# Eight blocks of a matrix-vector product move from TensorE to GpSimd, and three small tiles grow to 64 bytes

## The chip, the cores and the metric

One core of a Trainium2 chip runs the whole program. The metric is the device time of one execution in microseconds, the median of several runs. A profiled execution gives the trace, from which every row below is read.

## The reference

Two transformer blocks run one after the other on 512 tokens of width 1024; the first also carries 256 context tokens. What matters here is the first block's start:

```python
mod_lat = jnp.split((jax.nn.silu(c) @ w_mod[l] + b_mod[l])[:, None, :], N_MOD, axis=-1)   # w_mod: 1024 x 9216
mod_ctx = jnp.split(jax.nn.silu(c_ctx) @ w_mod[l] + b_mod[l], N_MOD, axis=-1)
x = ffn_sub(x, mod_lat[0:3], ...); s_ctx = ffn_sub(s_ctx, mod_ctx[0:3], ...)        # first feed-forward
h_lat = modulate(rmsnorm(x, norm2_w[l]), mod_lat[3], mod_lat[4])                    # and the same for the context
x = x + mod_lat[5] * lat_mix                                                       # after the mixer
x = ffn_sub(x, mod_lat[6:9], ...)                                                  # second feed-forward
```

So 9 vectors of 1024 numbers come from two matrix-vector products with one 37.7 MB matrix; vectors 0 to 2 are wanted by the first feed-forward, 3 and 4 just behind it, 5 after the mixer, 6 to 8 by the second feed-forward. The mixer holds an mLSTM scan and an HGRN2 scan. The second block holds a state-space mixer, sparse attention and a mixture of 32 experts.

## The kernel before

Everything is fp32. A large product is done as three fp32r matmuls (`mm3`, L210 to L212): the weights are split into a rounded part `whi` and a rest `wlo` (`wsplit`, L191 and L192), the activations into `lath`/`latl`, `ctxh`/`ctxl` and `hh`/`hl`. A feed-forward (`ffn`) takes the hidden width of 2816 in 22 slices of 128, in eight groups of 2, 2, 3, 3, 3, 3, 3, 3. A slice has two weight loads for its first product (outputs `pppa`, 512 columns for the latents, 256 for the context) and one for its second (outputs `pppb`). After each group one function of the list `fill` is called.

A block of the matrix-vector product (`matvec`, four columns of 128 outputs) loads 2 MB of weights in four DMAs on SP's queue, runs 8 fp32 matmuls with 32 columns of weights (L265; the trace has two records for each), copies the result out and turns and sums it with 4 matmuls (L275, eight records). `mod` has 18 such blocks, named here by their first column: 0 to 12 before the first feed-forward, 16 and 20 in `begin`, 24 to 36 after groups 0 to 3 of it, and 40 to 68 in the list `self.fill`, which also has four blocks of `w_ada_2`. From that list two are taken behind the feed-forward (`FT`, L2458), one ahead of each of the four heads of the mLSTM scan (`FB[0]`, L807), one in each of the four HGRN2 fronts (`FB[1]`, L940) and two at the end of these (`FB[2]`, L528). These come through the ordinary weight buffers `wraw`; the ones in the feed-forward through `mraw` (`MR` = 6 buffers).

Instructions are written in program order and a planner orders each engine's queue from that order and from modelled times; on the chip each queue then runs strictly in order. A DMA on SP's queue that waits for a buffer holds every DMA behind it.

Tiles are stacked: a pool takes addresses (bytes within a partition) upward from the pool below it, each tile rounded up to 32 bytes, and the pools `wp` (`wraw`, `whi`, `wlo`) and `tp` come down from the other end. In this program `whi` and `wlo` lie at 186336, 190432, ... and 198624, ..., all 32 above a multiple of 64. The constants begin at 16512, `eps` (4 bytes, takes 32) lies at 17760, and everything opened later lies on top: `lath` at 21504, `latl` at 37888, `ctxh` at 54272, all multiples of 64. `hh` and `hl` lie at multiples of 64 in the first feed-forward (125120, 128192, ...), and at 32 above one in the second (123104, 126176, ...), because there they sit on another stack, with `inv` (4 bytes, takes 32) under them. The last tile under the expert weights `ew` (123904, a multiple of 64) is `frs` (16 bytes, takes 32).

GpSimd has the lower halves of some normalised blocks (`norm_block`, L355 and L356, for k in 0, 3, 6) and work of the scans.

Of the kernel before, what the change touches and what calls it, by code (L numbers as in the profile page):

```python
# [10 lines left out]
F32 = mybir.dt.float32  # L11
# [5 lines left out]
OP = mybir.AluOpType  # L17
# [23 lines left out]
class Kern:  # L41
# [60 lines left out]
    def setup(self):  # L102
        nc, cst = self.nc, self.cst
        self.ident = cst.tile([128, 128], F32, name="ident")
        nc.sync.dma_start(self.ident, self.i["k_ident"])
        self.ones = cst.tile([128, 128], F32, name="ones")
        nc.vector.memset(self.ones, 1.0)
        self.sel4 = cst.tile([128, 32], F32, name="sel4")
        nc.sync.dma_start(self.sel4, self.i["k_sel4"])
        self.eps = cst.tile([128, 1], F32, name="eps")  # L110
        nc.vector.memset(self.eps, 1e-6)
        self.tiny = cst.tile([128, 1], F32, name="tiny")
        nc.vector.memset(self.tiny, 7.8e-20)

# [101 lines left out]
    mva = False  # L216
# [25 lines left out]
    def mvrows(self, p):  # L242
        if self.mvp is None:
            rows = self.tp.tile([128, 512], F32, name="mvr", tag="mvr", bufs=1)
            self.nc.scalar.copy(rows, p)
        else:
            rows = self.mvp.tile([128, 512], F32, name="mvs", bufs=2)
            (self.nc.scalar.copy if self.mva else self.nc.vector.tensor_copy)(rows, p)
        return rows

    def matvec(self, dst, w, sc, n, c0, nb, bias, tag=None):

# [225 lines left out]
HGL = 420  # L478
ZB = 6
EARLY = 200  # L480
FB = (1, 1, 2)
LV = [64, 32, 16, 8, 4, 2, 1]
QSC = 0.5 * 128 ** -0.5

# [641 lines left out]
class Mix2:  # L1126
# [3 lines left out]
    def rope_tables(self, i, pool, cosd, sind):  # L1130

        nc = self.nc
        inv = pool.tile([128, 1], F32, name="inv")
        nc.sync.dma_start(inv, i["k_invf"])
        pos = i["positions_2"][0]
        pf = self.tmp("posf")
        if pos.dtype == I32:
            raw = self.tmp("pos0").bitcast(I32)
            nc.sync.dma_start(raw[0:1, :], pos[None, :])
            nc.vector.tensor_copy(pf[0:1, :], raw[0:1, :])  # L1140
        else:
            p32 = pos.bitcast(I32)
            for r in range(2):
                raw = self.tmp("pos%d" % r).bitcast(I32)
                nc.sync.dma_start(raw[0:1, :], p32[r * 512:(r + 1) * 512][None, :])
                nc.vector.tensor_copy(pf[0:1, r * 256:(r + 1) * 256], raw[0:1, 0:512:2])
        p = self.pt("pb")
        nc.tensor.matmul(p, self.ones[0:1, :], pf[0:1, :], start=True, stop=True)
        ang = self.tmp("ang")
        nc.vector.tensor_scalar(ang, p, inv, None, op0=OP.mult)  # L1150
        MG = 12582912.0
        C1, C2, C3 = 6.28125, 1.9350051879882812e-03, 3.019916050561733e-07
        k = self.tmp("kk")
        nc.vector.tensor_scalar(k, ang, 1.0 / (2 * math.pi), MG, op0=OP.mult, op1=OP.add)
        nc.vector.tensor_scalar(k, k, MG, None, op0=OP.subtract)
        for c in (C1, C2, C3):
            nc.vector.scalar_tensor_tensor(ang, k, -c, ang, op0=OP.mult, op1=OP.add)

        ab = self.tmp("ab")
        nc.scalar.activation(ab, ang, AF.Abs)  # L1160
        s = self.tmp("sn")
        nc.vector.tensor_scalar(s, ab, -1.0, 3.14159274101257324, op0=OP.mult, op1=OP.add)
        nc.vector.scalar_tensor_tensor(s, s, -8.74227766e-08, ab, op0=OP.add, op1=OP.min)
        nc.scalar.activation(s, s, AF.Sin)
        sg = self.tmp("sg")
        nc.scalar.activation(sg, ang, AF.Sign)
        nc.vector.tensor_mul(s, s, sg)
        nc.sync.dma_start(sind, s)
        nc.vector.tensor_scalar(ab, ab, -1.0, math.pi / 2, op0=OP.mult, op1=OP.add)
        nc.scalar.activation(ab, ab, AF.Sin)  # L1170
        nc.sync.dma_start(cosd, ab)
# [786 lines left out]
class Moe:  # L1958
# [271 lines left out]
    def finish(self, mo, yac, yg, fg, out):  # L2230

        nc = self.nc
        ss = mo.tile([128, 4, 2], F32, name="fss")
        for c in range(4):
            for f in range(2):
                fs = slice(f * 512, f * 512 + 512)
                j = self.tmp("fj")
                nc.scalar.activation(j, yac[:, c, fs], AF.Square, accum_out=ss[:, c, f:f + 1])
                (nc.vector if f else nc.gpsimd).tensor_tensor(yg[:, c, fs], yac[:, c, fs], fg[:, fs], op=OP.mult)  # L2239
        r = mo.tile([128, 4], F32, name="frs")  # L2240
        nc.vector.tensor_add(r, ss[:, :, 0], ss[:, :, 1])
        nc.scalar.activation(r, r, AF.Ln, bias=self.eps, scale=1.0 / D)
        nc.scalar.activation(r, r, AF.Exp, scale=-0.5)
        for c in range(4):
            if c % 2:
                nc.scalar.activation(yg[:, c, :], yg[:, c, :], AF.Copy, scale=r[:, c:c + 1])
            else:
                nc.vector.tensor_scalar(yg[:, c, :], yg[:, c, :], r[:, c:c + 1], None, op0=OP.mult)
            nc.sync.dma_start(out[c * 128:(c + 1) * 128, :], yg[:, c, :])
# [73 lines left out]
LATE = 1500  # L2323
FT = (2,)
M0 = 16
MR = 6
FN = 6
FA = 2
MA = (0, 1)
# [22 lines left out]
class Top:  # L2352
# [41 lines left out]
    def first(self, i, b1, lat, mrg, xd, x1d, cosd, sind, row):  # L2394
        nc, tc, cst = self.nc, self.tc, self.cst
        wm = i["w_mod"][0]
# [22 lines left out]
        with tc.tile_pool(name="xp", bufs=1, reuse_waits="tile") as xp:  # L2419
# [5 lines left out]
            a, b = A("sA"), A("sB")  # L2425
# [8 lines left out]
            ada = b1.tile([128, 16, 1], F32, name="ada")  # L2434
            vec, g1 = {}, A("sG")

            def begin():
                mm(16)
                mm(20)
                gate(2, 0.5, 2, g1)  # L2440
                self.bada = self.columns("c", [("b", i["b_ada_2"][0], 48)])["b"]
                self.sc2 = self.silu_cols([i["c_2"]], "2")
                vec.update(self.columns("b", [("l0", i["hg_lb_logits"][0].rearrange("a b -> (a b)"), 8),
                                              ("l1", i["hg_lb_logits"][1].rearrange("a b -> (a b)"), 8),
                                              ("hgw", i["hg_norm_w"][0], 4), ("mlcw", i["ml_conv_w"][0], 36),
                                              ("mlcb", i["ml_conv_b"][0], 4)]))
                self.lower_bounds(vec["l0"], vec["l1"], vec)
                self.fill = [lambda b=b: mm(b) for b in range(40, 72, 4)]
                self.fill += [lambda b=b: self.matvec(ada[:, b:b + 4], i["w_ada_2"][0], self.sc2, 1, b * 128, 4,
                                                      self.bada[:, b:b + 4]) for b in range(0, 16, 4)]  # L2450
            g = g1
            with tc.tile_pool(name="mw", bufs=1, reuse_waits="tile") as self.mvp, \
                    tc.tile_pool(name="act", bufs=1, reuse_waits="tile") as self.act:
                self.ffn(i["ffn1_w1"][0], i["ffn1_w2"][0], hi, lo, [(0, L, xT, g[:, 0]), (L, C, xc, g[:, 1])],
                         self.ends(xT, g[:, 0]) + [(L, C, xc, g[:, 1])],
                         begin, [lambda b=b: mm(b) for b in range(24, 40, 4)])
            self.mvp = None
            self.fillers(FT[0])  # L2458
            a, b = scales(3, "n2")
# [116 lines left out]
```

## Time and profile before

| | us |
|---|---|
| median of 3 runs | 2839.8 (2837.2 to 2843.13) |
| profiled execution, its own time | 2847.28 |
| its span from first to last instruction | 2845.5 |
| TensorE (PE) busy | 2684.1 (94%) |
| VectorE (DVE) busy | 1553.9 (55%) |
| ScalarE (ACT) busy | 995.2 (35%) |
| GpSimd (POOL) busy | 280.4 (10%) |

Times of rows count from the start of the span. An engine's busy time is the union of its instructions; a matmul's end is modelled, so two matmuls in a row overlap in the list, and what one costs is the distance from its start to the next start. "L12" is line 12 of the kernel. In brackets behind a row of the order of time stands the idle time before the instruction, and what ended it.

### The profile page before, as it was taken

What the parts mean: (1) busy time and instruction counts of PE and PEld (TensorE: products, weight loads), DVE (VectorE), ACT (ScalarE), POOL (GpSimd) and SP (SyncE); (2) the same over time, 40 slices, a digit from 0 to 9 for tenths busy, and PEclk for the clock granted to TensorE, in tenths of its full rate; (3) what the DMA queues carried; (4) which work ended last, traced back from release to release, by engine and by line L of the source; (5) the groups of instructions that cost most, each with busy time, mean ns of one, the idle gap of its engine ahead of it and who ended that gap; (6) DMA issues with size and microseconds to landing.
All of it is one profiled execution on the core that took longest, in us unless ns stands there. A gap on an engine that the chain in (4) does not pass through costs nothing. (4 is left out here: it accounts for less than half of the span.)

```text
span 2845.5 us, 40809 instructions
## 1 busy us (share of the span) xinstructions
PE 2684.1 (94%) x16161; PEld 2052.9 (72%) x16162; DVE 1553.9 (55%) x3022; ACT 995.2 (35%) x1787; POOL 280.4 (10%) x319
## 2 busy tenths in 40 slices
PE   7999999999998887999999899999999989969997
PEld 5788888888887765678788678777777767854443
DVE  6333333338367895554435756676666664454444
ACT  5211112225235663422223424555444443231112
POOL 2000000003001220100000101121122220000000
PEclk8999999999999998999999999999999999979999
DMA  7422222134333228732333433201234367269995
GB/s 261 149 89 67 59 61 66 46 97 118 94 102 103 64 83 263 260 96 82 105 95 103 135 87 95 80 13 43 78 104 119 97 195 242 74 245 377 379 378 203
DMA packets 340996, 384.66 MB, mean 135 GB/s; under 512 B 20793, under 2 KB 251581, under 8 KB 340546
## 3 DMA queue, kind: packets, MB, share of 16 engines
q1 hardware_dynamic: 338498, 373.62, 40.7%
q0 software_dynamic: 2304, 8.39, 0.8%
q8 instruction: 129, 2.11, 0.3%
q14 instruction: 65, 0.53, 0.1%
HBM read 352.33 MB, written 29.63 MB: 134 GB/s over the span
## 5 line engine op out<-in xcount | busy, mean ns | idle before, releaser
L191 ACT CAST whi<-wraw 128x1024 fp32r<-128x1024 f32 x277 | 285.9, 1042 | 756.7 <-PE pppa L211 329.3
L210 PE MATMUL pppa<-lath,whi 128*128 128x512 f32 (+4 forms) x1344 | 523.1, 390 | 19.5 <-ACT lath L1833 5.4
L211 PE MATMUL pppa<-latl,whi 128*128 128x512 f32 (+3 forms) x1344 | 519.7, 387 | 5.1 <-DVE latl L358 3.0
L212 PE MATMUL pppa<-lath,wlo 128*128 128x512 f32 (+3 forms) x1344 | 513.2, 384 | 0.0
L192 DVE TENSOR_TENSOR wlo<-wraw,whi 128x1024 fp32r<-128x1024 f32 (+1 forms) x273 | 332.4, 1224 | 252.0 <-ACT whi L191 247.4
L210 PEld LDWEIGHTS pppa<-lath,whi 128*128 128x128 f32 (+3 forms) x1344 | 253.0, 188 | 87.4 <-ACT whi L191 11.9
L211 PEld LDWEIGHTS pppa<-latl,whi 128*128 128x128 f32 (+2 forms) x1344 | 252.6, 188 | 65.4 <-DVE latl L358 5.4
L212 PEld LDWEIGHTS pppa<-lath,wlo 128*128 128x128 f32 (+2 forms) x1344 | 252.1, 188 | 55.5 <-issue 2.5
L211 PE MATMUL pppb<-hl,whi 128*128 128x512 f32 (+1 forms) x576 | 195.3, 341 | 0.0
L210 PE MATMUL pppb<-hh,whi 128*128 128x512 f32 (+1 forms) x576 | 193.1, 344 | 0.0
L212 PE MATMUL pppb<-hh,wlo 128*128 128x512 f32 (+1 forms) x576 | 191.5, 341 | 0.0
L416 DVE SCALAR_TENSOR_TENSOR xT<-pppb,sG,xT 128x512 f32<-128x512 f32 (+1 forms) x144 | 96.7, 689 | 137.7 <-PE pppb L212 137.5
L396 DVE TENSOR_TENSOR hf<-sg,pppa 128x256 f32<-128x256 f32 (+1 forms) x68 | 39.7, 584 | 234.6 <-PE pppa L212 233.3
L210 PE MATMUL pppf<-lath,whi 128*128 128x512 f32 x320 | 128.9, 403 | 5.9 <-ACT lath L1833 2.2
L210 PE MATMUL pppa<-ctxh,whi 128*128 128x256 f32 (+1 forms) x440 | 125.1, 284 | 7.9 <-DVE W L919 7.9
L211 PE MATMUL pppf<-latl,whi 128*128 128x512 f32 x320 | 128.3, 401 | 0.8 <-DVE latl L1834 0.7
L2137 PE MATMUL pppa<-ew,xg 128*64 128x512 f32 x512 | 128.3, 607 | 0.0
L212 PE MATMUL pppf<-lath,wlo 128*128 128x512 f32 x320 | 127.4, 398 | 0.6 <-DVE wlo L192 0.6
L210 PEld LDWEIGHTS pppb<-hh,whi 128*128 128x128 f32 x576 | 108.0, 188 | 27.6 <-issue 5.8
L211 PE MATMUL pppa<-ctxl,whi 128*128 128x256 f32 (+1 forms) x440 | 124.6, 283 | 0.3 <-POOL ctxl L356 0.3
L212 PE MATMUL pppa<-ctxh,wlo 128*128 128x256 f32 (+1 forms) x440 | 124.7, 284 | 0.0
L211 PEld LDWEIGHTS pppb<-hl,whi 128*128 128x128 f32 x576 | 108.4, 188 | 16.1 <-issue 3.4
(697 smaller groups left out, 4999.6 us busy)
## 6 DMA issues: line engine op xcount, KB each, us to landing
wraw<-in_ffn_w_dram SPq DMA_DIRECT2D x132, 512.0 KB, 3.9
wraw<-in_w_in_dram SPq DMA_DIRECT2D x102, 512.0 KB, 4.0
ew<-in_w_exp_gate_dram SPq DMA_DIRECT2D x64, 512.0 KB, 8.0
ew<-in_w_exp_up_dram SPq DMA_DIRECT2D x64, 512.0 KB, 4.6
ew<-in_w_exp_down_dram SPq DMA_DIRECT2D x32, 1024.0 KB, 10.6
mraw<-in_w_mod_dram SPq DMA_DIRECT2D x40, 512.0 KB, 6.5
wraw<-in_w_mod_dram SPq DMA_DIRECT2D x32, 512.0 KB, 3.9
mraw<-in_w_ada_dram SPq DMA_DIRECT2D x32, 512.0 KB, 5.8
```

Of the source, the lines that this page charges most:

```text
L191: nc.scalar.copy(hi[:, :n], raw[:, :n])
L192: (nc.gpsimd if pool else nc.vector).tensor_sub(lo[:, :n], raw[:, :n], hi[:, :n].bitcast(F32))
L210: nc.tensor.matmul(out, wh, xh, start=start, stop=False)
L211: nc.tensor.matmul(out, wh, xl, start=False, stop=False)
L212: nc.tensor.matmul(out, wl, xh, start=False, stop=stop)
L396: nc.vector.tensor_mul(h[:, :n], sg[:, :n], pp[1])
L416: nc.vector.scalar_tensor_tensor(x[:, o, :], p[:, :n], gate[:, o:o + 1], x[:, o, :], op0=OP.mult, op1=OP.add)
L2137: nc.tensor.matmul(ph[x * 64:x * 64 + 64, :], xg[:, k, x * 64:x * 64 + 64], wts[k // 4 * 2 + x][:, :, k % 4, :], start=(k == 0), stop=(k = ...
```

## The change

`matvec_pool` does a block on GpSimd: each row of the weights' 128x512 tiles is multiplied by the vector's entry of its partition and added up, for both vectors; what is left is a sum over the 128 partitions, which TensorE does with a column of ones. Blocks 24 to 52 go that way, one after each of the eight groups of the first feed-forward; each one's last step is written behind the next one's GpSimd work, the last one's behind the feed-forward. The list `self.fill` starts at 56, and the scan's heads take none of it (`FB[0]` = 0). `MR` is 4. `eps`, `inv` and `frs` are made 64 bytes wide, of which the same first columns are used.

```diff
-        self.eps = cst.tile([128, 1], F32, name="eps")
-        nc.vector.memset(self.eps, 1e-6)
+        eps = cst.tile([128, 16], F32, name="eps")
+        nc.vector.memset(eps, 1e-6)
+        self.eps = eps[:, :1]
...
+    def matvec_pool(self, dst, w, sc, n, c0, bias):
+        nc = self.nc
+        acc = [self.mvp.tile([128, 512], F32, name="mva", bufs=4) for _ in range(n)]
+        for i in range(4):
+            a = self.cols(w, c0, 512)
+            a = bass.AP(tensor=a.tensor, offset=a.offset + i * 256 * w.shape[1], ap=[a.ap[0], [a.ap[1][0], 2], a.ap[2]])
+            v = self.mvraw(a)
+            for k in range(2):
+                j = 2 * i + k
+                for m in range(n):
+                    col = sc[:, j, m:m + 1]
+                    if j == 0:
+                        nc.gpsimd.tensor_tensor(acc[m], v[:, k, :], col.to_broadcast([128, 512]), op=OP.mult)
+                    else:
+                        t = self.mvp.tile([128, 512], F32, name="mvt", bufs=2)
+                        nc.gpsimd.tensor_tensor(t, v[:, k, :], col.to_broadcast([128, 512]), op=OP.mult)
+                        nc.gpsimd.tensor_tensor(acc[m], acc[m], t, op=OP.add)
+        def rest():
+            p = self.pt(self.ptag)
+            for q in range(4):
+                for m in range(n):
+                    nc.tensor.matmul(p[:, q * n + m:q * n + m + 1], acc[m][:, q * 128:(q + 1) * 128], self.ones[:, 0:1],
+                                     start=True, stop=True)
+            nc.vector.tensor_tensor(dst, p[:, :4 * n].rearrange("p (b m) -> p b m", m=n),
+                                    bias[:, :, None].to_broadcast([128, 4, n]), op=OP.add)
+        return rest
...
-FB = (1, 1, 2)
+FB = (0, 1, 2)
...
-        inv = pool.tile([128, 1], F32, name="inv")
+        inv = pool.tile([128, 16], F32, name="inv")[:, :1]
...
-        r = mo.tile([128, 4], F32, name="frs")
+        r = mo.tile([128, 16], F32, name="frs")[:, :4]
...
-MR = 6
+MR = 4
...
+            open_ = []
+            def late(b):
+                open_.append(self.matvec_pool(mod[:, b:b + 4], wm, sc, 2, b * 128, v1["b"][:, b:b + 4]))
+                if len(open_) > 1:
+                    open_.pop(0)()
...
-                self.fill = [lambda b=b: mm(b) for b in range(40, 72, 4)]
+                self.fill = [lambda b=b: mm(b) for b in range(56, 72, 4)]
...
-                         begin, [lambda b=b: mm(b) for b in range(24, 40, 4)])
+                         begin, [lambda b=b: late(b) for b in range(24, 56, 4)])
+                open_.pop()()
```

## Rows read from the trace of the kernel before

**Rows 1.** Busy time by stretch: length, each engine's busy us (instructions), granted clock, DMA share, GB/s.

```profile
100.00:620.00 520.00, 518.29 (x2916) 435.97 (x2911) 182.55 (x267) 101.35 (x142) 1.74 (x4) 1.00 0.23 71
764.70:799.00 34.30, 31.95 (x268) 16.28 (x267) 15.20 (x62) 12.45 (x33) 0.00 (x0) 0.90 0.79 248
799.00:860.00 61.00, 60.16 (x447) 56.83 (x444) 42.54 (x130) 23.35 (x73) 0.00 (x0) 0.92 0.22 60
860.00:1130.00 270.00, 229.97 (x2658) 180.60 (x2656) 216.21 (x452) 151.75 (x243) 49.71 (x56) 0.94 0.40 122
1200.00:1545.00 345.00, 342.02 (x1502) 275.79 (x1501) 149.22 (x183) 88.38 (x111) 0.00 (x0) 1.00 0.32 94
2000.00:2400.00 400.00, 374.61 (x1754) 283.10 (x1753) 259.54 (x409) 172.22 (x247) 91.15 (x88) 0.98 0.46 139
```

**Rows 2.** The same view for lines L265, then L275, alone, in the first feed-forward.

```profile
100.00:620.00 520.00, 16.60 (x60) 2.28 (x54) 1.00 0.23 71
100.00:620.00 520.00, 3.79 (x32) 3.91 (x32) 1.00 0.23 71
```

**Rows 3.** Order of time on PE: turning one block, and the matmul behind it.

```profile
335.65 0.95 PE L275 MATMUL pppa<-sel,mvs 128*128 128x2 f32 x8
336.46 0.48 PE L210 MATMUL pppa<-lath,whi 128*128 128x512 f32 x1
```

**Rows 4.** Busy time of L265, then L275, in the scan's stretch; then PE there.

```profile
764.70:799.00 34.30, 14.85 (x64) 2.03 (x64) 0.90 0.79 248
764.70:799.00 34.30, 4.21 (x32) 3.87 (x32) 0.90 0.79 248
...
770.59 1.92 PE L265 MATMUL pppa<-wraw,scm 128*32 128x512 f32 x4 [1.19 <-DMA wraw<-in_w_mod_dram]
799.06 0.39 PE L555 MATMUL pppa<-whi,lath 128*128 128x256 f32 x1
```

**Rows 5.** SP's queue in order of time: start, time to the last issue, DMAs.

```profile
715.48 71.32 SPq L181 DMA_DIRECT2D wraw<-in_w_mod_dram  x16
789.75 9.65 SPq L181 DMA_DIRECT2D wraw<-in_w_in_dram  x6
```

**Rows 6.** GpSimd instructions with two inputs of 128x512: duration min/median/max in ns.

```profile
L1747 POOL TENSOR_TENSOR W<-W,cb x32: 1267/1314/2146, 2025.3 to 2321.6; 128x512 f32<-128x512 f32 x32
L1773 POOL TENSOR_TENSOR ysa<-ysa,ysq x8: 1268/1290/1295, 2077.6 to 2328.9; 128x512 f32<-128x512 f32 x8
```

**Rows 7.** DVE groups with both inputs in SBUF, 100 to 620 us: count, busy us, mean ns.

```profile
L192 DVE TENSOR_TENSOR wlo<-wraw,whi 128x1024 fp32r<-128x1024 f32 x59 | 71.4, 1224 | 61.1 <-ACT whi L191 61.0
L398 DVE TENSOR_TENSOR hl<-hf,hh 128x512 fp32r<-128x512 f32 x20 | 13.8, 692 | 13.1 <-ACT hh L397 13.1
L398 DVE TENSOR_TENSOR hl<-hf,hh 128x256 fp32r<-128x256 f32 x19 | 8.1, 426 | 9.0 <-ACT hh L397 9.0
```

**Rows 8.** A weight load on SP's queue; the split of the first one's weights on ACT.

```profile
254.84 18.82 SPq L181 DMA_DIRECT2D wraw<-in_ffn_w_dram  x5
271.00 1.05 ACT L191 CAST whi<-wraw 128x1024 fp32r<-128x1024 f32 x1 [1.75 <-PE pppa L211]
```

**Rows 9.** PE groups by shape, 130 to 600 us, then 1200 to 1545 us.

```profile
L211 PE MATMUL pppb<-hl,whi 128*128 128x512 f32 x136 | 53.7, 395 | 0.0
L211 PE MATMUL pppa<-ctxl,whi 128*128 128x256 f32 x295 | 82.3, 279 | 0.0
...
L211 PE MATMUL pppa<-latl,whi 128*128 128x512 f32 x324 | 128.0, 395 | 0.0
L211 PE MATMUL pppb<-hl,whi 128*128 128x512 f32 x152 | 59.2, 390 | 0.0
L211 PE MATMUL pppb<-hl,whi 128*128 128x256 f32 x23 | 6.4, 283 | 0.0
```

**Rows 10.** PE in order of time: eight steps in the first, nine in the second feed-forward.

```profile
337.91 0.40 PE L210 MATMUL pppa<-lath,whi 128*128 128x512 f32 x1
339.78 0.39 PE L212 MATMUL pppa<-lath,wlo 128*128 128x512 f32 x1
...
1221.35 0.39 PE L212 MATMUL pppb<-hh,wlo 128*128 128x512 f32 x1
1223.39 0.39 PE L212 MATMUL pppb<-hh,wlo 128*128 128x512 f32 x1
```

**Rows 11.** GpSimd's first instruction behind the first feed-forward.

```profile
640.26 1.09 POOL L355 TENSOR_SCALAR nu<-nt,sB 128x256 f32<-128x256 f32 x1 [326.54 <-PE pppb L212]
```

## The prediction, made before the result was known

> **What bounds the kernel now.** I read the table of stretches first. In the first feed-forward PE is busy 518.3 of 520 us at full clock, in the second 342.0 of 345, while DVE works a third of the time and GpSimd 1.7 us [rows 1]: there, a microsecond taken from PE is a microsecond of the span, and GpSimd is free. In the scan's stretch, 764.7 to 799, DMA is busy 79% at 248 GB/s, thirty points above any other row, and the clock is 0.90 [rows 1]. The order of time says why: PE waits for weights of the product itself (1.19 us before one group of L265), SP's queue spends 715 to 787 us on 16 loads of `w_mod`, and only then, at 789.75, on the `w_in` loads whose matmuls (L555) start at 799.06 [rows 4, 5]. So four blocks that were meant as filling hold the stretch up. From 860 to 1130 PE is busy only 230 of 270 us, from 2000 to 2400 375 of 400 [rows 1]: a gain on PE counts only partly there.
>
> **The change, part 1: four blocks out of the feed-forward's TensorE work.** L265 there costs 16.6 us [rows 2]. Turning a block takes from 335.65 to 336.46, 0.81 us for eight records [rows 3]; four blocks 3.2 us. Removed: 19.8 us. Added: `rest` has 4 x 2 matmuls of 128 weight columns with one column moving; the nearest row is L275, same weights with two columns, two records for each matmul, so 16 records or 1.6 us, and for all eight blocks (they all end in or behind this feed-forward) 13.0 us. Net -6.8 us. Had one column cost half of two, it would be -13; had every first weight load of a group of its own cost 0.25 us more, -5.
>
> **Part 2: four blocks out of the scan.** L265 and L275 are busy 14.85 + 4.21 us of the 34.3, with small overlaps; from start to next start I count 18.0 us [rows 4]. What is left of PE's work there is 14.2 us, and a chain of small DVE and ACT steps, DVE 15.2 and ACT 12.5 us long [rows 1], which does not get shorter. What fills PE instead are the 192 matmuls of L555 to L557 behind it, 22 us at the 117 ns from start to start that 256 columns take (part 4): they depend on the normalised tokens alone, and their loads no longer stand behind 16 others. Lower bound of the gain: 0, the chain lasts its 34 us whatever PE does. Upper bound: the 18.0 us, the 2.3 us of gaps between the matmuls, and half of the 61 us x (1 - 0.92) / 0.5 = 10 us at half clock behind it [rows 1], 25 us in all. I take 18, since the fill is there, the stretch is 79% DMA and that load goes.
>
> **Part 3: GpSimd's own work.** A block has 2 + 7 x 2 x 2 = 30 instructions of 128x512, eight blocks 240. The rows for two inputs of that shape have medians of 1.290 and 1.314 us, the longest 2.146 us beside DVE work [rows 6]: 42 us (1.4 each, my choice) a block, 336 in all, at worst 64 and 515. Groups last some 48 us (two slices) or 72 us (three), so GpSimd keeps up in either case. With two accumulators for each of two blocks, a block must wait for the `rest` of the one before the last, which is written one group later: about a group of slack. The last block starts when group 6 ends and is done before group 7 is, and the norm that wants GpSimd at 640.26 [rows 11] finds it free. Vectors 3 and 4 (blocks 24 to 36) are ready long before. Cost on GpSimd: nothing. Cost of sharing: DVE's instructions with both inputs in SBUF are 71.4 + 13.8 + 8.1 us recorded in 520 [rows 7], about 100 with those missing from the trace. The 2.146 us row shows that a GpSimd instruction can wait; I let DVE wait likewise. DVE goes from 35% to at most 60%, and its late `hl` can hold a group's second product: bounds 0 and 8 x 1.3 = 10 us, I take 3.
> [...]
>
> **The queue it is moved past.** 32 loads of 512 KB go to `mraw` as before, 16 of them earlier than before, at 0.23 DMA share. With four buffers a load waits until GpSimd has done 8 instructions, 10.5 to 17 us, and weights behind it on SP's queue wait too. A weight load is issued at 254.84 and split at 271.00, 16 us later, when PE gives up a buffer [rows 8]. So a load may come some 12 us late at no cost (0 taken). The planner knows GpSimd's speed only by its model; if that is too fast, this slack goes.
>
> **Part 4: 32 bytes.** `eps` takes 64 bytes instead of 32, so every tile above it moves by 32: `lath`, `latl`, `ctxh`, `ctxl`, `mh`, `y0h` and the first feed-forward's `hh` go from a multiple of 64 to 32 above one, where `whi` and `wlo` lie. The second feed-forward's `hh` is there already, moves by 64 (`eps` and `inv`) and stays so. That makes before a measurement of it: the same line, shape and stage gives 395 ns for `latl` at 0 and 390 ns for `hl` at 32; in the first feed-forward `hl` at 0 has 395 [rows 9]. In starts: eight steps of `lath` take 1.87 us, 0.234 each, nine of `hh` at 32 take 2.04, 0.227 [rows 10]. Over all records at full clock, paired with the program's addresses, I get 233.4 against 227.5 ns. With 256 columns it goes the other way: `ctxl` at 0 279 ns, `hl` at 32 283 [rows 9]; in starts 117.2 against 119.9. Counted in the program, 5232 matmuls of 512 columns move from 0 to 32 beside weights at 32: -5.8 x 5232 = -30.3 us. Of 256 columns 2664 move: +2.7 x 2664 = +7.2; and 768 where the weights are the moving side (L555 to L557): +1 at most. Net -22; I take -20 for the stretches in which PE is not the bound. Ends: 0, if it is not the place that makes the difference between the two feed-forwards, and -30. `frs` takes 32 bytes more, which puts `ew` and what follows back on a multiple of 64: the last stage stays as it is, 0.
> [...]
>
> **Sum.** -6.8 - 18 + 3 - 20 = -41.8 us on the profiled 2847.28, whose span is 2845.5; the profiled execution is 7.5 us above the median of 2839.8. Taken off the median: **2798 us**, its own range 2780 to 2814.
>
> **Rivals.**
> 1. Place does nothing (the 395 and 390 come from the context's matmuls in between, which only the first feed-forward has). For it: one stage is all that shows the fast value. Against: `latl` in the second feed-forward has no context either and is at 395 [rows 9]. -6.8 - 18 + 3 = -22: 2818 us. Chance 0.13.
> 2. The scan is bound by its chain: PE idles where the four blocks were. For it: DVE and ACT are together busy 27.7 of 34.3 us. Against: 79% DMA share, the wait for `w_mod`, `w_in` loads at 789.75 [rows 1, 4, 5]. -6.8 + 3 - 20 = -24: 2816 us. Chance 0.15.
> 3. Slower: GpSimd holds SP's queue. Every GpSimd instruction takes 2.146 us [rows 6], a buffer comes free after 17.2 us instead of the planned 10.5, each block's four loads are late by 4 x 6.7 = 27 us, and beyond the 16 us that a weight load has in hand [rows 8], PE stands still 11 us a block, 86 us in all: -42 + 86 = +44, 2884 us. It decides when lateness in a block goes over 16 us, and it outweighs the rest from 5.3 us of standstill a group on. For it: the order is fixed by a model, and DVE shares. Against: the median is 1.31, DVE is busy a third. Chance 0.08.
> 4. Both 1 and 2, about -4: 2836 us, 0.04.
>
> **How the numbers follow.** The forecast has 0.60, the rivals 0.40. The range for 8 in 10 reaches from the low ends of parts 2 to 4 together (-6.8 - 25 + 0 - 30 = -62) to halfway between rivals 1 and 2 and rival 4: 2778 to 2826. A measurement can't tell less than 0.2%, 5.7 us. Faster: 0.60 + 0.13 + 0.15 = 0.88; same: rival 4 and a mild form of rival 3, 0.05; slower 0.07.
>
> **What would show it.** GpSimd with some 240 instructions of 1.3 to 1.5 us between 90 and 640, without a `nu` behind the feed-forward that waits for it; no L265 between 110 and 620, and 16 records of `rest` eight times. The first `nu` behind the feed-forward some 8 us earlier than 640.26 (part 1 with 3 lost, part 4 with 4.3). 512-column groups of `lath` at 390 ns as `hl` is now, 256-column ones of `ctxh` at 283. From 760 to 860 some 18 us less, with L555 among the scan's matmuls and no `w_mod` loads before it. The second feed-forward 5 to 6 us shorter. Wrong it would be if PE waits for ACT's `whi` in the first feed-forward (rival 3), if PE has idle time of 15 us or more in the scan (rival 2), or if `lath` stays at 395 (rival 1).

## The result, and the profile after

The changed kernel takes 2950.85 us (median of 4 runs, 2948.31 to 2953.4), the kernel before 2841.47 on the same chip: ratio 1.0373, interval [1.035, 1.0395]. Forecast were 2798 us and "faster". The profiled execution took 2948.31 us, its span 2946.6.

From the page: share and instructions of four engines, and TensorE's granted clock in 40 slices.

```profile
PE 2663.8 (90%) x16097; PEld 2070.0 (70%) x16098; DVE 1679.4 (57%) x3018; ACT 994.8 (34%) x1783; POOL 551.7 (19%) x559
...
PEclk8889899999999899999999999999999999979999
```

PE works 20 us less than before and the span is 101 us longer: PE stands still. Where, the same view as [rows 1] says, for the first feed-forward (which now reaches to 720) and for the scan from its first transposition of `bm` to its output:

```profile
100.00:720.00 620.00, 501.17 (x2815) 435.68 (x2816) 306.55 (x264) 97.16 (x136) 268.16 (x241) 0.90 0.23 72
888.50:985.70 97.20, 83.20 (x660) 76.41 (x659) 56.98 (x183) 31.34 (x98) 2.40 (x1) 0.91 0.14 39
```

In the feed-forward PE is busy 501 of 620 us, where [rows 1] had 518.3 of 520. DVE's busy time has gone up although DVE got no work there. On the way through the program the execution is 117.8 us behind before at the DMA of `xd` that follows the feed-forward's end (645.3 before, 763.1 now), 127.4 at the scan's end, 111.0 at the start of the second feed-forward, 101.1 at the end. So the loss is made in the first feed-forward, some more up to the scan's end, and the rest of the program gives 26 us back.

The view of waits from 100 to 720 (us in all, times, longest) and the groups there:

```profile
PEld pppa L214 <- DVE wlo L194: 114.6, 7, 26.5
PE pppa L214 <- DVE wlo L194: 113.1, 7, 26.3
...
L194 DVE TENSOR_TENSOR wlo<-wraw,whi 128x1024 fp32r<-128x1024 f32 x57 | 190.4, 3359 | 54.5 <-ACT whi L193 54.5
L270 POOL TENSOR_TENSOR mva<-mva,mvt 128x512 f32<-128x512 f32 x112 | 141.8, 1287 | 0.0
L269 POOL TENSOR_TENSOR mvt<-mraw,scm 128x512 f32<-128x512 f32 x112 | 114.6, 1044 | 9.7 <-DMA mraw<-in_w_mod_dram 9.7
```

Seven waits of PE make 113 us, all for `wlo`, DVE's rest of the weights. Its mean is 3359 ns, against 1224 in [rows 7]. Read the seven in the order of time, here the third:

```profile
296.89 2.55 POOL L270 TENSOR_TENSOR mva<-mva,mvt 128x512 f32<-128x512 f32 x2
299.40 2.04 POOL L269 TENSOR_TENSOR mvt<-mraw,scm 128x512 f32<-128x512 f32 x2
301.40 2.50 POOL L270 TENSOR_TENSOR mva<-mva,mvt 128x512 f32<-128x512 f32 x2
...
300.54 0.48 DVE L447 SCALAR_TENSOR_TENSOR xc<-pppb,sG,xc 128x256 f32<-128x256 f32 x1 [0.32 <-PE pppb L214]
300.94 14.91 DVE L194 TENSOR_TENSOR wlo<-wraw,whi 128x1024 fp32r<-128x1024 f32 x1
...
315.90 0.79 PE L214 MATMUL pppa<-lath,wlo 128*128 128x512 f32 x1 [13.14 <-DVE wlo L194]
316.49 0.63 PE L212 MATMUL pppa<-lath,whi 128*128 128x512 f32 x1
316.92 0.63 PE L213 MATMUL pppa<-latl,whi 128*128 128x512 f32 x1
```

GpSimd runs a block's 30 instructions without a gap, a train from 281.4 to 314.8. `wlo` is issued at 300.94 in the middle of it and ends at 315.85, one microsecond behind the train's end: it did nearly all of its 1.22 us of work only when GpSimd was through. The other six are the same: 26.7, 30.0, 14.9, 14.9, 14.9 and 13.0 us, each ending 1.1 us behind a train (the two longest behind trains of 44 instructions, one block and half of the next). Products that read one operand from PSUM (`xc<-pppb`, 0.48 us, as in the median before) run inside the train as ever. Behind each standstill the matmuls are 0.43 us apart instead of 0.23: the granted clock is 0.50 there, here from 303.8 to 320.8, and 1.00 from 320.8 to 330. PE's standstills from 102 us to the end of the feed-forward sum to 117.5 us (1.7 before); the 4.4 that are not for `wlo` are for `whi`.

### The profile page after: what moved, and what is told of

Read it like the earlier page. It is cut to its first block, busy times and chain, and to the rows that moved or that the text cites. A ratio compares the mean times of both kernels' runs of the same rounds, so it can differ in the third digit from the quotient of the medians.

```text
span 2946.6 us, 40929 instructions
## 1 busy us (share of the span) xinstructions
PE 2663.8 (90%) x16097; PEld 2070.0 (70%) x16098; DVE 1679.4 (57%) x3018; ACT 994.8 (34%) x1783; POOL 551.7 (19%) x559
## 5 line engine op out<-in xcount | busy, mean ns | idle before, releaser
L194 DVE TENSOR_TENSOR wlo<-wraw,whi 128x1024 fp32r<-128x1024 f32 (+1 forms) x273 | 454.9, 1674 | 253.1 <-ACT whi L193 244.7
L212 PE MATMUL pppa<-lath,whi 128*128 128x512 f32 (+3 forms) x1344 | 527.5, 393 | 12.9 <-ACT whi L193 5.9
L212 PEld LDWEIGHTS pppa<-lath,whi 128*128 128x128 f32 (+2 forms) x1344 | 258.2, 192 | 79.3 <-ACT whi L193 13.0
L270 POOL TENSOR_TENSOR mva<-mva,mvt 128x512 f32<-128x512 f32 x112 | 141.8, 1287 | 0.0
```

Of the source, the lines that this page charges most:

```text
L194: (nc.gpsimd if pool else nc.vector).tensor_sub(lo[:, :n], raw[:, :n], hi[:, :n].bitcast(F32))
L212: nc.tensor.matmul(out, wh, xh, start=start, stop=False)
L270: nc.gpsimd.tensor_tensor(acc[m], acc[m], t, op=OP.add)
```

## Experiments

Theory: DVE's instructions with two SBUF inputs are kept out while GpSimd's train reads SBUF. Rivals: the loads and buffers of the sums (the prediction's third rival), GpSimd's busy time as such, the new order. "Ends" below is the `xd` DMA behind the first feed-forward: 645.3 before, 763.1 changed.

**The parts alone.** `e1_place`: before with the three wider tiles only. `e2_pe` and `e3_dve`: the changed kernel with the eight blocks on TensorE and on DVE. `e2_pe` also has `MR` = 6 again, so not everything else is as changed there; `e3_dve` keeps 4.

```diff
-  [lambda b=b: late(b) for b in range(24, 56, 4)]        # e2_pe
+  [lambda b=b: mm(b) for b in range(24, 56, 4)]
...
-  nc.gpsimd.tensor_tensor(t, v[:, k, :], col.to_broadcast([128, 512]), op=OP.mult)     # e3_dve
-  nc.gpsimd.tensor_tensor(acc[m], acc[m], t, op=OP.add)
+  nc.vector.scalar_tensor_tensor(acc[m], v[:, k, :], col, acc[m], op0=OP.mult, op1=OP.add)   # j = 0: tensor_scalar, mult
```

> The kernel before with eps, inv and frs made 64 bytes wide and nothing else. Theory (the place of a tile within 64 bytes sets the pace of a matmul): in the changed kernel's trace the stages behind the scan are 2.7 (second feed-forward), 2.8, 2 and 3 us shorter than before, and lath's 512-column steps are at 226 to 232 ns instead of 234. Alone it should give 12 to 22 us off: 2841 goes to 2819 to 2829. Rival (these stages are shorter for another reason, such as the order of the queues): within 3 us of before.

> The changed kernel with blocks 24 to 52 on TensorE in the first feed-forward, as before has four of them; everything else (the list, no fill in the scan's heads, the places) stays changed. Theory (the loss is DVE's wlo standing still while GpSimd works): the 117 us of PE standstill in the first feed-forward are gone, eight blocks at 4.95 us instead of four add 20, the rest is as in the changed kernel (17 us shorter from the feed-forward's end to the last instruction): 2835 to 2845. The scan from bm to mrs stays at 97 us, 3 above before. Rival (the loss comes from where the blocks and their loads stand in the order, not from GpSimd): 2900 to 2950.

> The changed kernel with the sums of the eight blocks on DVE: one scalar_tensor_tensor (weight times entry plus sum) takes the place of GpSimd's multiplication and addition, 128 instructions instead of 240. Theory (the port pair between DVE and GpSimd is the loss): no GpSimd work, no wlo above 2 us; the 128 instructions at some 0.75 us (the row of the product with one input in PSUM) are 96 us of DVE, which is idle for half of the 520 us; the feed-forward is 5 to 11 us shorter than before, the rest 17: 2810 to 2825. If the 16 instructions of a block stand ahead of a wlo in DVE's queue (12 us), PE stands still up to 10 us a block: 2890. Rival (the loss comes from the loads and buffers of the sums): 2900 to 2950.

| | us | ratio to before | ends |
|---|---|---|---|
| e1_place | 2826.28 | 0.993 [0.9911, 0.9948] | 640.2 |
| e2_pe | 2848.28 | 1.0014 [1.0003, 1.0025] | 658.8 |
| e3_dve | 2818.72 | 0.9908 [0.989, 0.9926] | 635.5 |

The places give 17.5 us. Without GpSimd the loss is gone, in e3_dve with the same loads and buffers as in the change: PE's standstills are 4.2 us there and none in e2_pe. e2_pe came 3 us above its range. The "port pair" of e3_dve's expectation and the "port" of later ones are assumptions: the runs show which instructions wait for which and for how long, not through what.

**GpSimd without reading SBUF.** `t3_memset` replaces the arithmetic by memsets.

```diff
-  nc.gpsimd.tensor_tensor(t, v[:, k, :], col..., op=OP.mult); nc.gpsimd.tensor_tensor(acc[m], acc[m], t, op=OP.add)
+  nc.gpsimd.memset(t, 0.0); nc.gpsimd.memset(t, 0.0); nc.gpsimd.memset(acc[m], 0.0); nc.gpsimd.memset(acc[m], 0.0)
```

> The changed kernel with GpSimd's multiplications and additions replaced by memsets of the same 128x512 tiles (two for each, 0.55 us each by the 128x660 row of the trace of before, so trains of some 33 us), and one copy of 128x2 for each load: the sums of blocks 24 to 52 are left out. Theory (GpSimd's reads of SBUF and DVE's second SBUF input exclude each other): no wlo above 2.5 us, PE has no standstill, 2825 to 2845. Rival (any GpSimd work on SBUF, or its place in the queues and the loads of mraw, holds the feed-forward up): wlo of 10 to 30 us as now, 2940 to 2960.

A copy of two columns for each load stays. It took 3019.13 us, but with vectors 3 to 6 left out the numbers that reach the experts are others, and the last stage is 177 us longer (that the experts get other tokens is the likely reason, not shown); up to the load of the first expert weights it is level with before (2458.0 against 2462.8). The feed-forward ends at 645.3. The row of `wlo` (minimum/median/maximum in ns):

```profile
L194 DVE TENSOR_TENSOR wlo<-wraw,whi x59: 1215/1225/1229, 130.7 to 617.0; 128x1024 fp32r<-128x1024 f32 x59
```

Trains of memsets keep no `wlo` waiting, though GpSimd is busy 185.9 us from 100 to 640, so what keeps DVE out is not that GpSimd works but its multiplications and additions, which read SBUF.

**Shorter trains, other neighbours.** `e4_spread` writes the work in 64 pieces behind the weight loads; `t2_twice` lets ACT round each `whi` twice.

```diff
+                    w1t[s] = self.wsplit(...); step()      # e4_spread: one 256 KB load, 2 or 4 instructions
...
+            nc.scalar.copy(hi[:, :n], raw[:, :n])           # t2_twice, ahead of the same line
```

> The changed kernel with GpSimd's work of a block cut into eight pieces of 2 or 4 instructions (one 256 KB load each), one piece written behind each of 64 weight loads of the feed-forward, so that its loads come in the pace of the weights. GpSimd does the same 240 instructions of 1.04 and 1.29 us. Theory (DVE stands still until GpSimd's train ends, whatever its length): the longest train is 4.7 us, the longest wlo some 6 us, and as wlo is 6 to 14 us ahead of PE inside a group and 2 at its end, PE stands still 0 to 25 us in all: 2815 to 2850. Rival (each GpSimd instruction takes its share, so that the loss goes with GpSimd's 268 busy us): PE stands still some 117 us as now: 2930 to 2960.

> The changed kernel with ACT's rounding of a weight block (whi) done twice in the first feed-forward, so that wlo can start 1.04 us later and DVE is idle for about 0.8 us ahead of it where it now follows xc<-pppb at once. Theory B (no idle time ahead of it keeps wlo out): the long waits vanish, PE waits some 1 us more at each of eight group ends: 2840 to 2860. Theory A (a predecessor that reads PSUM) and C (the train as such): the long waits stay, 2945 to 2965. If t1_small and this one both lose the waits, a gap or another instruction is enough.

e4_spread: 2921.69 us, ends at 717.3; t2_twice: 2991.56, ends at 769.3. Both lie outside every range named ahead. In e4_spread the pieces ran together again, as loads came faster than GpSimd worked (trains of 31 to 40 us), and six `wlo` took 7.5 to 16.8 us. In t2_twice DVE was idle 2.0 to 2.6 us ahead of each of the seven `wlo`, and they waited all the same (10 to 28 us): theory B fell. (It also rounds twice in the second feed-forward, 20 us there against the change.) A third kernel, `t1_small` (2970.42 us, ends at 772.0), was to have a small memset of DVE ahead of each `wlo`; they were all ordered to the front of the queue, the seven long waits stayed, and it told nothing of theory A. But e4_spread showed what the change's long trains never did: inside a train, some got in.

```profile
244.28 1.66 DVE L194 TENSOR_TENSOR wlo<-wraw,whi 128x1024 fp32r<-128x1024 f32 x1 [1.58 <-ACT whi L193]
247.00 2.18 DVE L194 TENSOR_TENSOR wlo<-wraw,whi 128x1024 fp32r<-128x1024 f32 x1 [1.06 <-ACT whi L193]
...
243.83 3.02 POOL L269 TENSOR_TENSOR mvt<-mraw,scm 128x512 f32<-128x512 f32 x2
246.81 3.52 POOL L270 TENSOR_TENSOR mva<-mva,mvt 128x512 f32<-128x512 f32 x2
```

Here GpSimd waits for DVE: 3.02 us for two instructions that take 2.04 undisturbed. All such cases lay in a group's first half, where `hl` and `wlo` come at most 10 us apart; all long waits in its second half, 19 us or more into a train.

**When DVE gets in.** `t4_ticks` and `t7_big` add small two-input instructions of DVE in the second half; `t6_early` moves six trains into the first (with `MR` = 3).

```diff
+                    nc.vector.tensor_tensor(dum, x[:, o, :16], x[:, o, 16:32], op=OP.add)     # t4_ticks
+                    nc.vector.tensor_tensor(dum, x[:, o, :], x[:, o, :], op=OP.add)           # t7_big
...
+                    if fill and f == fb + 2 and s == 0: fill.pop(0)()                         # t6_early
```

> The changed kernel with a DVE addition of two 16-column pieces of xT (both in SBUF) behind every second product xT<-pppb, so that DVE asks for two SBUF inputs some every 6 us in a group's second half and not first after 19 to 26 us of an undisturbed GpSimd train. Theory D (a DVE instruction that asks early or often gets in between two GpSimd instructions, as the hl and wlo of a group's first half do at 0.4 to 2.3 us; one that comes when GpSimd has run undisturbed for about 19 us or more is kept out to the end): each addition waits 1.3 us at most, wlo too, no wait above 3 us, 2835 to 2860. Theory C (in a group's second half GpSimd's train keeps DVE out whenever it asks): the additions themselves stand still to the train's end, and earlier than wlo does: 2960 to 3050.

> Six blocks (32 to 52) on GpSimd, each started in the first half of a group of three slices (behind its fifth weight load), where hl and wlo come at most 10 us apart, and blocks 24 and 28 on TensorE. Theory D (DVE gets in if it asks often): the six trains of 33 us each pass within the 50 us of that half, no wait above 3 us, the first feed-forward ends near 642 us (635.5 with eight blocks on DVE, plus two blocks at 3.4), total 2820 to 2835. Rival (a GpSimd train keeps DVE out wherever it lies): six waits of 10 to 30 us, 2900 or more.

> The changed kernel with a DVE addition of 128x512 with both inputs in SBUF (0.69 us) behind every second product xT<-pppb of the first feed-forward, about every 6 us, where t4_ticks had 16 columns; GpSimd's work as in the changed kernel. In all traces so far DVE got in where it came up to 12.4 us behind a train's start or behind the last time that it had held a GpSimd instruction up, and was kept out from 15.1 us on; 16 columns slipped in without holding GpSimd up. Theory D (time or count of undisturbed GpSimd instructions decides): each addition holds GpSimd up, the next comes 6 us later, no wait above 3 us, PE stands still under 20 us: 2835 to 2865. Rival (in a group's second half a train closes some 15 us after its start, whatever DVE did): the third addition of each group stands still for 12 to 15 us, 2945 to 2970.

t4_ticks: 2954.96, ends at 752.6. t6_early: 2853.13 (1.0028 [1.0013, 1.0044]), ends at 643.8. t7_big: 2845.32 (0.9996 [0.9982, 1.0011]), ends at 638.1. The three additions of one group, first in t4_ticks (its train from 259.6), then in t7_big (from 303.8):

```profile
265.79 0.36 DVE L450 TENSOR_TENSOR dum<-xT 128x16 f32<-128x16 f32 x1
271.95 1.22 DVE L450 TENSOR_TENSOR dum<-xT 128x16 f32<-128x16 f32 x1
278.11 14.89 DVE L450 TENSOR_TENSOR dum<-xT 128x16 f32<-128x16 f32 x1
```

```profile
310.06 1.12 DVE L450 TENSOR_TENSOR dum<-xT 128x512 f32<-128x512 f32 x1
316.33 1.05 DVE L450 TENSOR_TENSOR dum<-xT 128x512 f32<-128x512 f32 x1
322.61 0.95 DVE L450 TENSOR_TENSOR dum<-xT 128x512 f32<-128x512 f32 x1
...
310.59 2.99 POOL L270 TENSOR_TENSOR mva<-mva,mvt 128x512 f32<-128x512 f32 x2
```

The 16-column additions slip in without holding GpSimd up (twice), and 18.5 us into the train the third stands still to its end. The 512-column ones hold GpSimd up (2.99 us for 2.58) at the same places, and none is shut out: the longest `wlo` is 2.3 us, PE's standstills 6.6 us, with 240 GpSimd instructions as in the change. Theory A falls here too: each addition comes 0.04 us or less behind a product that reads PSUM, and gets in. So what shuts DVE out is that GpSimd's train has run on undisturbed, in time or in number of instructions, and not the half of the group. Over the twelve traces with trains, counted from the train's start or from where DVE last held it up, DVE gets in up to some 12 us and is shut out in about 50 cases from some 15 us on, save where a memset stood next and save four instructions in the first train of t4_ticks, which got in at 15 to 24; the bounds are rough, since what counts as held up is a choice. Why is open.

t4_ticks lies outside both of its ranges; of theory C it bears out the third addition of a group, not the first two. t6_early has no `wlo` above 2.3 us, as expected; its total missed, and not by its trains. From the scan's last product with `cst` and `qs` to the second feed-forward's first with `hh`, where no train runs, the change takes 341.6 us and e3_dve 340.6, but t6_early 366.9, t7_big 363.5, e4_spread 363.7 and t2_twice 363.7. Some 20 us of these four totals come from there; the reason was not followed.

**Letting DVE in.** A memset of 128x256 in GpSimd's train: ahead of every multiplication (`t5_open`), once for a load (`k1_piece`), once for a block (`k2_once`).

```diff
+                        nc.gpsimd.memset(t[:, :256], 0.0)                                    # t5_open
+                        if (k == 0 or i == 0) and m == 0: nc.gpsimd.memset(t[:, :256], 0.0)  # k1_piece
+                        if j == 6 and m == 0: nc.gpsimd.memset(t[:, :256], 0.0)              # k2_once
                         nc.gpsimd.tensor_tensor(t, v[:, k, :], col.to_broadcast([128, 512]), op=OP.mult)
```

> The changed kernel with a memset of 128x256 on GpSimd (0.31 us by the 128x258 row of before) ahead of each multiplication into mvt, so that GpSimd reads nothing from SBUF for 0.3 us after every 2.3 us; blocks get 8.8 us longer. Theory (a GpSimd instruction that does not read SBUF gives the port back, as the memset trains let every wlo through): wlo waits at most 2.5 us, PE stands still under 20 us in the first feed-forward, 2830 to 2860. Rival (a train keeps DVE out as long as one GpSimd instruction follows another, whatever is between): long waits as now or some 9 us longer each, 2950 to 3030.

> The changed kernel with one memset of 128x256 on GpSimd ahead of every load's work (about every 8 to 11 instructions), a quarter of t5_open's. So far 33 DVE instructions with two SBUF inputs were kept out to a train's end, all of them 18.5 us or more after the train began or after DVE last held it up, and nearly all that came sooner got in after one GpSimd instruction. Theory (a train becomes closed only after some 18 us, and a memset begins it anew): every wlo gets in within 2.5 us, the first feed-forward ends near t5_open's 634 us, 2815 to 2830. Rival (DVE gets in only where a memset is directly next): waits up to 10 us behind a memset's distance, PE stands still 30 to 60 us, 2850 to 2885.

> The changed kernel with a single memset of 128x256 in each block's 30 instructions, ahead of the last load's work, some 25 us behind the train's start. In the changed kernel wlo asks at 19.5 us and stands still 14.9 us to the train's end at 33.4. Theory (the memset gives the port to a waiting DVE): wlo of the regular trains lasts about 7 us (to the memset), the train goes on behind it, PE stands still about 5 us a group instead of 13: 2865 to 2895. Rival (once shut out, DVE waits for the train's end): 14.9 us again, 2945 to 2960.

| | us | ratio to before | ends | PE's standstill in the feed-forward |
|---|---|---|---|---|
| changed | 2950.85 | 1.0373 [1.035, 1.0395] | 763.1 | 117.5 |
| k2_once | 2860.3 | 1.0052 [1.0029, 1.0075] | 675.5 | 35.6 |
| k1_piece | 2843.25 | 0.9991 [0.9976, 1.0006] | 662.8 | 21.5 |
| t5_open | 2822.24 | 0.9918 [0.9893, 0.9943] | 634.0 | 4.4 |

More work on GpSimd (332 us busy in t5_open, 268 in the change), 129 us off the program, and t5_open is below its range. The memset lets in a DVE instruction that is already shut out. In k2_once `wlo` asks at 268.87 and gets in at the one memset (6.02 us for two, of which the first is 4.04); GpSimd then waits for it. The one long wait left there, 22.5 us from 175.67, also ends at the next memset.

```profile
268.87 6.02 DVE L194 TENSOR_TENSOR wlo<-wraw,whi 128x1024 fp32r<-128x1024 f32 x2
...
271.75 0.33 POOL L270 MEMSET mvt<- 128x256 f32 x1
272.02 3.77 POOL L271 TENSOR_TENSOR mvt<-mraw,scm 128x512 f32<-128x512 f32 x2
```

But it does not begin the train anew: in k1_piece seven `wlo` lasted 4.5 to 5.7 us, until the next memset, though in six of them one had run 5.6 to 5.8 us earlier. There my theory was wrong and the rival right in kind; the time, 2843.25 us, lies between their two ranges.

**The best of it.** Four blocks instead of eight, and the scan's heads with their blocks as before: on DVE (`w2_dve4`), on GpSimd with a memset for each load (`g4_piece4`) or for each multiplication (`g5_open4`); `w3_dve8` keeps eight on DVE and takes the list's later blocks for the heads.

```diff
-FB = (0, 1, 2)
+FB = (1, 1, 2)
...
-  self.fill = [lambda b=b: mm(b) for b in range(56, 72, 4)]       # not in w3_dve8
+  self.fill = [lambda b=b: mm(b) for b in range(40, 72, 4)]
-  [lambda b=b: late(b) for b in range(24, 56, 4)]
+  [lambda b=b: late(b) for b in range(24, 40, 4)]
```

> The places as changed, four blocks (24 to 36) summed on DVE in the first feed-forward, and blocks 40 to 52 back in the list with one for each head of the scan, as before. Theory: against the places alone (2826) four blocks of L265 and L275 go from the first feed-forward (19.8 us) and four times the closing product comes (6.5), 13 us off: 2810 to 2816, and against eight blocks on DVE (2819) 3 to 9 us less, since the scan does not gain from losing its four blocks. Rival (the scan's blocks cost what they take): 2825 to 2835.

> Eight blocks on DVE in the first feed-forward as in e3_dve (2819), with one block of the list again ahead of each head of the scan. Theory (the heads are bound by small DVE and ACT steps, TensorE's blocks there are hidden work): the 8 us that e3_dve loses from bm to mrs against the places alone come back, the HGRN2 stretch has two blocks fewer to hide, 2806 to 2816. Rival (the scan is no different): 2817 to 2821.

> The places as changed, four blocks (24 to 36) on GpSimd with one memset for each load, and blocks 40 to 52 back in the list with one for each head of the scan, as in w2_dve4 (2812) which has the four on DVE. Theory (with the port given back, GpSimd's work is free): the same as w2_dve4 within 0.2%, 2806 to 2818. Rival (GpSimd's sharing costs DVE 1 us at each wlo and these reach PE): 2818 to 2826.

> As g4_piece4 (four blocks on GpSimd, the places as changed, the list with one block for each head), with the memset of 128x256 ahead of every multiplication into mvt, as in t5_open. Theory (with the port given back every 2.3 us GpSimd's blocks cost the first feed-forward nothing): no wlo above 2.5 us, the feed-forward ends within 3 us of w2_dve4's 628 us, 2808 to 2820. Rival (GpSimd's sharing still reaches TensorE, beyond the waits): the feed-forward ends at 634 or later, 2821 to 2835.

w2_dve4: 2812.19 us, 0.9892 [0.9869, 0.9914], ends at 627.9. It beats both kernels and has the lowest median of all; its interval overlaps those of e3_dve, w3_dve8 and t5_open, so that it beats these is not shown. w3_dve8: 2819.95, 0.9909 [0.9892, 0.9926], no better than e3_dve, as its rival said: from `bm` to the scan's end it takes 92.8 us against 96.1, but the HGRN2 stretch got longer. g4_piece4: 2830.85, 0.9944 [0.9922, 0.9966], outside both its ranges, ends at 638.7 with three `wlo` of 5 us. g5_open4: 2822.69, 0.9928 [0.9914, 0.9942], ends at 628.7: within 1 us of the same blocks on DVE, so in the feed-forward GpSimd's work is free once it lets DVE in. Its total is in the rival's range all the same, 3 us above its own. In the profiled executions it is 5 us behind w2_dve4 at the last instruction, lost from the scan on; why is open.

## Why the prediction was wrong

**Part 3, the cost of sharing, is the step that failed.** It let a DVE instruction wait as long as one GpSimd instruction (2.146 us, [rows 6]) and took 3 us, 10 at most. The price of one meeting was not one instruction but the rest of a train, 13 to 30 us, seven times; with PE's 2 us of lead on `wlo` at a group's end (it asks at 300.94 above, PE wants it at 302.76), nearly all of it reached PE. e3_dve, the same program without trains, ends at 635.5, the change at 763.1: 127.6 us, of which 113.3 are standstill (117.5 less 4.2); the other 14 fit the lower clock behind it (an estimate: in the seven stretches at a granted clock of 0.50 PE is busy 30 us behind its standstills, and at 0.43 us a step for 0.23 some 14 of them are lost). The row of 2.146 us came from a stage, 2000 to 2400, where GpSimd runs at most three instructions in a row (5.55 us from 2064.35), and says nothing of 30.
Which pairs exclude each other, the runs show: `wlo`, with two SBUF inputs, lasts up to 29.95 us in the change beside GpSimd's arithmetic on SBUF and 1229 ns at most beside memsets in t3_memset, and `xc<-pppb` takes 0.48 us inside a train. That the one kept out gets in when one GpSimd instruction ends, as the prediction took it, they do not show: `wlo` at 200.51 stood still through some 25 of them. The prediction priced single waits for DVE and never asked whether one could go on into the next instruction.

**GpSimd's own time** was right at the low end: 1.04 and 1.29 us an instruction, 33.4 us a block (42 taken), and it kept up. (A group of three slices lasts 77 us in the trace of before, not the 72 of the prediction; nothing hangs on it.)

**The queue it is moved past** (0) held: SP waited 95.3 us in thirteen turns for GpSimd (66.5 in nine for L269, 28.8 in four for L266) to free a buffer, and PE waited for `whi` 4.4 us in all, 0.9 at most. So rival 3, the only one on the slower side, had the side but not the mechanism: PE waited for `wlo`, not for `whi`.

**Part 1** (-6.8) was right in kind: against the places alone, e3_dve ends 4.7 us earlier, w2_dve4 (four blocks out, four `rest` in, no other move) 12.3, where the same sum gives 13.3.

**Part 2** (-18) failed too, and rival 2 is near what happened. From `bm` to the scan's end:

```profile
757.40:848.20 90.80, 87.86 (x704) 71.11 (x704) 57.67 (x190) 34.12 (x103) 0.00 (x0) 0.94 0.43 134
```

```profile
746.20:837.90 91.70, 88.37 (x721) 70.20 (x721) 57.47 (x190) 34.48 (x104) 1.83 (x1) 0.98 0.43 133
```

```profile
758.90:855.00 96.10, 82.04 (x660) 75.34 (x659) 57.23 (x183) 31.12 (x98) 2.40 (x1) 0.93 0.14 39
```

These are e1_place and w2_dve4, which have the four blocks there, and e3_dve, which has not. DMA falls from 0.43 to 0.14, PE has 6 us less to do, DVE's and ACT's work is nearly the same, and the stretch is 5 us longer. Counted further, from the end of the first feed-forward to the start of the second, e3_dve takes 556.1 us and e1_place 558.5: the 5 us come back in the HGRN2 stretch, and the blocks' leaving is worth 2 us, not 18. That fits heads that are bound by their chain of small DVE and ACT steps; no run changed the chain itself, so this cause is argued. The 79% DMA share and the wait of 1.19 us for a weight [rows 1, 4] were true and did not bound the stretch. (The half clock in the upper bound is there: in the trace of before the granted clock is 0.50 from 803 to 811 us, and 1.00 from 820 to 860.) In the change the matmuls that were to fill the gap came too early (the last of L586 starts at 915.5, 21 us before the heads begin), and PE then idles, 14 us of the stretch.

**Part 4** (-20) was right in size, -17.5 us measured alone, but not in its rule. Steps of `lath` and `latl` went from 234 to 229 ns in the median, 5 of the 5.8 that it took; the +7.2 for 256 columns did not come (117 ns in the median for `ctxl`, as before; 113 in the change); and of the 24.6 us by which PE's busy time fell, 17.5 show in the total. The rule was that the place within 64 bytes counts, 32 above a multiple being the fast one beside weights that lie so. Two runs made for another purpose contradict it. In t1_small and t4_ticks a 64-byte tile `dum` lies under `lath`, which then starts at 21600 and not at 21536: within 64 the same, beside the same weights. The second feed-forward, first in e1_place, then in t4_ticks (before: 395 and 390 [rows 9]):

```profile
L213 PE MATMUL pppa<-latl,whi 128*128 128x512 f32 x312 | 122.3, 392 | 0.0
L213 PE MATMUL pppb<-hl,whi 128*128 128x512 f32 x151 | 59.1, 391 | 0.0
```

```profile
L213 PE MATMUL pppa<-latl,whi 128*128 128x512 f32 x312 | 123.2, 395 | 0.0
L213 PE MATMUL pppb<-hl,whi 128*128 128x512 f32 x152 | 60.1, 395 | 0.0
```

In starts, stretches of 141 steps of `lath` and `latl` there take 228.9 ns a step in e1_place and in the change, 232.4 or 233.3 in t4_ticks, 232.4 in t1_small and 233.3 before; `hl`, 32 above a multiple of 64 in all of them, is at 227 ns before, 229 in e1_place and 233 in t4_ticks (medians). From the second feed-forward's start to the first load of `ew` t1_small and t4_ticks take 1250.6 and 1251.3 us, as before (1250.5), and the change 1240.1. So place does count (rival 1 fell), over more than 64 bytes, and that the prediction came so near was in part luck; which rule holds is open.

## What to carry to other kernels

Before work goes to an idle GpSimd, look up which of DVE's instructions read two operands from SBUF, and how soon behind them PE stands: one instruction that meets a train without a gap can cost the rest of the train (11.2 to 26.3 us of PE's time each in the change). Do the sum on DVE if it has room (w2_dve4), or put short memsets (128x256, 0.33 us in k2_once) between GpSimd's instructions, closely: one for every two left PE 4.4 us of standstill (t5_open), one for each block 35.6 (k2_once). And "PE waits for a load here" does not say that the stretch is bound by loads: take the work out in one run and look whether the chain gets shorter (here four blocks less were worth 2 us, not 18).

## What the hardware showed that I had not expected

- A DVE instruction with two SBUF inputs is kept out by GpSimd's train for up to 29.95 us in the change, but, with four exceptions in t4_ticks, only once the train has run some 15 us undisturbed; before that it gets in soon (a `wlo` of 1.22 us then lasts 2.3 at most).
- A GpSimd memset of 0.33 us lets it in (k2_once: `wlo` asks at 268.87, the memset runs at 271.75, and GpSimd's next two instructions take 3.77 us for 2.04); a DVE instruction that holds GpSimd up every 6 us keeps the train open (t7_big, longest `wlo` 2.3 us), a 16-column one does not (t4_ticks, where the third lasts 14.89).
- Moving `lath` by 32 bytes takes 5 ns off a 512-column fp32r matmul (234 to 229, e1_place); 64 bytes more give most or all of it back (232 to 233, t1_small and t4_ticks). A 256-column one of `ctxl` stays at 117 in e1_place and is at 113 in the change.
